# Two tile pools change places in SBUF, and six extra tiles move into the larger one

## The chip, the cores and the metric

One NeuronCore of a Trainium2 chip. The metric is the device time of one execution, in microseconds (us). PE is the TensorE (PEld its weight loads), DVE the VectorE, ACT the ScalarE, POOL the GpSimd, SP the SyncE.

## The reference

Two layers on a sequence of 512 tokens of 1024 channels. Each layer is a SwiGLU feed-forward network (FFN) at half weight, a mixer (causal pooling in the first layer, multi-head latent attention in the second), and another such FFN. The four FFNs are most of the work:

```python
def swiglu(h, w_gate, w_up, w_down):
    return (jax.nn.silu(h @ w_gate) * (h @ w_up)) @ w_down
...
    for i in range(DEPTH):
        h = rmsnorm(x, ffn1_norm[i])
        x = x + FFN_HALF * swiglu(h, ffn1_w_gate[i], ffn1_w_up[i], ffn1_w_down[i])
        h = rmsnorm(x, mix_norm[i])
        ...
        h = rmsnorm(x, ffn2_norm[i])
        x = x + FFN_HALF * swiglu(h, ffn2_w_gate[i], ffn2_w_up[i], ffn2_w_down[i])
```

D_MODEL is 1024, D_FF 2816, everything float32.

## The kernel before

**Arithmetic.** A float32 product is made of three matmuls in float32r: each operand is split into a high part (ACT, L117) and a low part (DVE, L118), and `mm3` issues high x high, high x low and low x high (L110 to L112, all through the helper at L106). In `mm(ps, lhsT, rhs)` the first operand is the stationary one (128x128, loaded by an LDWEIGHTS before each matmul) and the second is the moving one, 256, 384 or 512 columns wide. A trace row names both: in `acc<-slot,hi` the moving operand is a tile `slot`, the stationary one a tile `hi`.

**FFN.** The 22 column tiles of gate and up are worked in four chunks (4, 6, 6, 6). Chunk 0 multiplies plainly, with 512 moving columns, and so do all down projections and the mixers' input and output projections. In chunks 1 to 3 a pair of column tiles and a pair of halves of the tokens are multiplied as 2x2 blocks with seven products instead of eight (class `Two`). Each product is 12 matmuls of 256 columns: four slices k of the channels, three matmuls each. Their numbers in the code are 1 to 7, and their order in one round is 5, 1, 4, 7, 6, 3, 2 (`twos`).

**Where the operands of the seven products stand.** Moving: the normalized activations `xn` and their block sums `ts`, high and low, 32 tiles of 128x512 in all, of which 26 are tiles `slot` of the pool `sp`. The other six come from `extra()` (L307): tiles named `t` in the FFN's own pool `fp`, for `xn[7]` and for the sums of k = 0. So products 7, 6, 5 and 4 begin with three matmuls whose moving operand is a `t`, and products 3 and 2 end with three. Stationary: the high and low parts for products 1, 2, 5 and 6 stand in the pool `wp` (tags `whi`, `wlo`), those for 3, 4 and 7 in `fp` (tags `chi`, `clo`, `dhi`, `dlo`). All other products have weights from `wp` and moving operands from `sp`, or, in the pooling layer and the attention, the other way about.

**Where the pools stand.** A pool takes a stretch of each SBUF partition in the order in which the pools are opened. The program as built has these offsets, in bytes of a partition; the last column is the remainder of the matmul operands' offsets by 512:

| pool | what | from | to | remainder by 512 |
|---|---|---|---|---|
| `sp` | 39 tiles `slot`, 2048 B each | 22944 | 102816 | 416 |
| `wp` | `raw`, `whi`, `wlo`, three tiles of 4096 B each | 102816 | 139680 | 416 |
| `kp`, `tp` | work tiles, small tiles (2884 B of them) | 139680 | 163044 | |
| `fp` | FFN's own: `s`, `chi`, `clo`, `m`, `t`, `dhi`, `dlo`, `z` | 163072 | 228608 | 256 |
| `mp` (instead of `fp` in the attention) | `vhi`, `vlo` and others | 163072 | 213984 | 480 for `vhi`, `vlo` |

The slices inside a tile are multiples of 512 B, so a matmul's operand has its tile's remainder.

Of the kernel before, what the change touches and what calls it, by code (L numbers as in the profile page):

```python
# [10 lines left out]
F32R = mybir.dt.float32r  # L11
# [7 lines left out]
P = 128  # L19
D = 1024  # L20
S = 512
FF = 2816
KD = D // P
# [54 lines left out]
def trunk(ctx: ExitStack, tc: tile.TileContext, a: dict, out: bass.AP):  # L78
# [1 line left out]

    cp = ctx.enter_context(tc.tile_pool(name="cp", bufs=1))
    xp = ctx.enter_context(tc.tile_pool(name="xp", bufs=1))
    sp = ctx.enter_context(tc.tile_pool(name="sp", bufs=39))
    wp = ctx.enter_context(tc.tile_pool(name="wp", bufs=3))
    kp = ctx.enter_context(tc.tile_pool(name="kp", bufs=2))
    tp = ctx.enter_context(tc.tile_pool(name="tp", bufs=2))
    pa = ctx.enter_context(tc.tile_pool(name="pa", bufs=6, space=PSUM))
    pb = ctx.enter_context(tc.tile_pool(name="pb", bufs=2, space=PSUM))

# [6 lines left out]
    def slot(shape=None):  # L96
        return sp.tile(shape or [P, S], F32R, tag="slot", name="slot")
# [16 lines left out]
    def split(src, hi, lo, scale=None):  # L114

        if scale is None:
            nc.scalar.activation(hi, src, AF.Copy)  # L117
            nc.vector.tensor_tensor(out=lo, in0=src, in1=hi.bitcast(F32), op=ALU.subtract)  # L118
        else:
            nc.scalar.activation(hi, src, AF.Copy, scale=scale)  # L120
            nc.vector.scalar_tensor_tensor(  # L121
                out=lo, in0=src, scalar=scale, in1=hi.bitcast(F32), op0=ALU.mult, op1=ALU.subtract
            )

    def load_w(src, cols):
        raw = wp.tile([P, WC], F32, tag="raw", name="raw")
        hi = wp.tile([P, WC], F32R, tag="whi", name="whi")
        lo = wp.tile([P, WC], F32R, tag="wlo", name="wlo")
        nc.sync.dma_start(raw[:, :cols], src)
        split(raw[:, :cols], hi[:, :cols], lo[:, :cols])  # L130
        return hi, lo
# [129 lines left out]
    def ffn(n, layer, prep, nxt, first=False, final=False):  # L261
        wg, wu, wd = (a[f"ffn{n}_{k}"] for k in ("gate", "up", "down"))
        with tc.tile_pool(name="fp", bufs=1) as fp:
            ffn_in(fp, wg[layer], wu[layer], wd[layer], prep, nxt, first, final)

    def ffn_in(fp, wg, wu, wd, prep, nxt, first, final):
# [37 lines left out]

        xn, ts, kept = [None] * KD, {}, []

        def extra():  # L307
            return fp.tile([P, S], F32R, tag="t", name="t", bufs=6)

        def normed(k):  # L310

            tag, dt = (("s", F32), ("s", F32), ("chi", F32R), ("clo", F32R))[k]
            both = fp.tile([P, 2 * S], dt, tag=tag, name=tag, bufs=2)
            both = both.bitcast(F32) if dt is F32R else both
            kept.append(both)
            for e, j in enumerate((k, KH + k)):
                t = both[:, e * S : (e + 1) * S]
                nc.vector.scalar_tensor_tensor(
                    out=t, in0=xs[j], scalar=gains[:, prep.gcol + j : prep.gcol + j + 1],
                    in1=rows, op0=ALU.mult, op1=ALU.mult,  # L320
                )
                xn[j] = (extra(), extra()) if j == KD - 1 else (slot(), slot())
                split(t, *xn[j])

        def x_sums(k):

            b12, b11, b22, b21 = (kept[k][:, c * C : (c + 1) * C] for c in range(4))
            t = fp.tile([P, 4 * C], F32, tag="m", name="m", bufs=2)
            t1, t2, t3, t4 = (t[:, c * C : (c + 1) * C] for c in range(4))
            for out, x, y in ((t1, b12, b11), (t2, b22, t1), (t3, b22, b12), (t4, b21, t2)):  # L330
                nc.vector.tensor_tensor(out=out, in0=x, in1=y, op=ALU.subtract)
            for e in range(2):
                new = extra if k == 0 else slot
                hi, lo = new(), new()
                split(t[:, e * S : (e + 1) * S], hi, lo)
                ts[k, 2 * e] = hi[:, :C], lo[:, :C]
                ts[k, 2 * e + 1] = hi[:, C:], lo[:, C:]
# [119 lines left out]
        for f0, f1 in CHUNKS:  # L457
            hs = []
            for f in range(f0, min(f1, 4), 2):
                if first and f == 0:  # L460
                    pg, pu = opening(wg[0], wu[0], prep)
                else:
                    pg = product(wg[f], xh)
                    if f == 0:
                        prep.squares()
                    if f == 2:
                        normed(0)
                    pu = product(wu[f], xh)
                    if f == 2:
                        normed(1)  # L470
                if rows is None:
                    r = prep.rstd()
                qg = product(wg[f + 1], xh)
                if rows is None:
                    rows = prep.rstd_rows(r)
                zs = scaled(pg), scaled(pu)
                if f == 2:
                    normed(2)
                hs.append(gated([(slice(0, S), zs[0])], zs[1]))
                qu = product(wu[f + 1], xh)  # L480
                if f == 2:
                    x_sums(0)
                zs = scaled(qg), scaled(qu)
                if f == 2:
                    normed(3)
                hs.append(gated([(slice(0, S), zs[0])], zs[1]))
# [9 lines left out]
            for m in range(KD):  # L496
                if f0 == 0 and m % 2 and m > 1:
                    x_sums(m // 2)
                hi, lo = load_w(wd[m][:, f0 * P : f1 * P], nf * P)

                nc_ = 2 if final and f1 == NFT and m == KD - 1 else 1
                for e in range(nc_):
                    p = acc()
                    cs = slice(e * S // nc_, (e + 1) * S // nc_)
                    for f in range(nf):
                        fs = slice(f * P, (f + 1) * P)
                        h = hs[f][0][:, cs], hs[f][1][:, cs]
                        mm3(p[:, cs], (hi[:, fs], lo[:, fs]), h, f == 0, f == nf - 1)
                    nc.vector.scalar_tensor_tensor(  # L509
                        out=xs[m][:, cs], in0=p[:, cs], scalar=0.5, in1=xs[m][:, cs],  # L510
                        op0=ALU.mult, op1=ALU.add,
                    )
                    if final and f1 == NFT:
                        nc.sync.dma_start(out[m][:, cs], xs[m][:, cs])
                if f1 == NFT and not final:
                    nxt.add(m)
# [669 lines left out]
```

## Time and profile before

| | |
|---|---|
| median of 3 runs | 1661.75 us (1661.46 to 1661.96) |
| the profiled execution's own time | 1661.68 us |
| its span, first to last instruction | 1659.9 us |
| granted TensorE clock over the span | 1.00 (2.4 GHz) |
| PE busy | 1649.3 us, 99% of the span |

A matmul's duration in the profile reaches from its start to a modelled end, and consecutive matmuls overlap. So the pace is read from the starts: the time from one matmul's start to that of a later one, divided by the matmuls between. "Pace" has that meaning below.

### The profile page before, as it was taken

Reading aid. Unit: us, or ns where it says so; the run is one execution under the profiler, and the core shown is the slowest. Engines: PE = TensorE matmul, PEld = TensorE weight load, DVE = VectorE, ACT = ScalarE, POOL = GpSimd, SP = SyncE. Lnnn points to the kernel's source line nnn. Section 1 sums busy time; section 2 is a strip of 40 time slices with the busy share of each in tenths; the row PEclk is TensorE's granted clock in tenths of the full one; section 3 lists DMA queues with packets and bytes.
Section 4 is the critical chain, followed back from the end, with each engine's and each line's share of the span. In section 5 each row is a group of like instructions: output and inputs, shape, how many; then the busy total and the mean of one; then the engine's idle time right before and its main releaser. Section 6 shows DMA issues by size and latency. Waiting matters only on the chain.

```text
span 1659.9 us, 26442 instructions
## 1 busy us (share of the span) xinstructions
PE 1649.3 (99%) x10534; PEld 1497.7 (90%) x10534; DVE 1246.0 (75%) x2082; ACT 823.6 (50%) x1411; POOL 47.6 (3%) x133
## 2 busy tenths in 40 slices
PE   8999999999999999999999999999999999999999
PEld 6898999988898989988999999888888889999898
DVE  8985758799976757669858677656778799677673
ACT  6453535455553535445535445446765455445351
POOL 0000000000000000000000000003321000000000
PEclk9999999999999999999999999999999999999999
DMA  5333333231434233332333333331112223333432
GB/s 167 104 116 111 100 89 118 84 114 57 121 102 118 85 112 99 98 96 83 124 92 115 89 115 96 103 88 53 45 58 77 76 65 127 90 115 96 121 90 89
DMA packets 52827, 161.74 MB, mean 97 GB/s; under 512 B 6240, under 2 KB 7008, under 8 KB 52704
## 3 DMA queue, kind: packets, MB, share of 16 engines
q1 hardware_dynamic: 52128, 159.34, 31.9%
q8 instruction: 82, 1.34, 0.3%
q10 hardware_dynamic: 576, 0.72, 0.1%
q14 instruction: 41, 0.34, 0.1%
HBM read 157.94 MB, written 2.10 MB: 96 GB/s over the span
## 4 chain that ended last, share of the span: by engine, by line
PE 95%; DVE 3%; ACT 1%; DMA 1%; issue 0%; SPq 0%; POOL 0%; ACTq 0%; DVEq 0%; POOLq 0%
PE acc L106 92%; PE aux L700 1%; PE aux L106 1%; DVE wlo L118 1%; PE aux L981 1%; DVE x L509 0%; DVE slot L121 0%; DVE sqacc L182 0%; DMA x<-in_xT 0%; DVE s L354 0%; DMA raw<-in_ffn_gate 0%; DMA raw<-in_ffn_up 0%; DMA freq<-in_freq 0%; ACT whi L117 0%; ACT work L962 0%
## 5 line engine op out<-in xcount | busy, mean ns | idle before, releaser
L106 PE MATMUL acc<-slot,whi 128*128 128x512 f32 x2204 | 679.5, 390 | 5.2 <-ACT whi L117 5.1
L106 PE MATMUL acc<-slot,hi 128*128 128x256 f32 x3168 | 582.2, 281 | 0.0
L106 PEld LDWEIGHTS acc<-slot,hi 128*128 128x128 f32 x3168 | 491.8, 190 | 0.9
L106 PEld LDWEIGHTS acc<-slot,whi 128*128 128x128 f32 x2204 | 411.0, 188 | 89.7 <-ACT whi L117 5.5
L106 PE MATMUL acc<-slot,lo 128*128 128x256 f32 x1584 | 446.4, 282 | 0.0
L106 PE MATMUL acc<-slot,wlo 128*128 128x512 f32 x1094 | 425.5, 389 | 0.0
L117 ACT ACTIVATE whi<-raw 128x768 fp32r<-128x768 f32 (+2 forms) x197 | 169.3, 862 | 300.4 <-PE acc L106 205.0
L106 PEld LDWEIGHTS acc<-slot,lo 128*128 128x128 f32 x1584 | 300.1, 189 | 0.1
L118 DVE TENSOR_TENSOR wlo<-raw,whi 128x768 fp32r<-128x768 f32 (+2 forms) x196 | 190.8, 977 | 102.1 <-ACT whi L117 99.8
L106 PEld LDWEIGHTS acc<-slot,wlo 128*128 128x128 f32 x1094 | 205.8, 188 | 43.3 <-DVE wlo L118 1.3
L118 DVE TENSOR_TENSOR lo<-s,hi 128x1024 fp32r<-128x1024 f32 x144 | 175.8, 1221 | 65.4 <-ACT hi L117 65.4
L117 ACT ACTIVATE hi<-raw 128x512 fp32r<-128x512 f32 (+1 forms) x144 | 121.3, 845 | 136.8 <-PE acc L106 84.1
L117 ACT ACTIVATE hi<-s 128x1024 fp32r<-128x1024 f32 x144 | 152.2, 1058 | 65.6 <-PE acc L106 59.4
L509 DVE SCALAR_TENSOR_TENSOR x<-acc,x 128x512 f32<-128x512 f32 x129 | 88.3, 684 | 127.5 <-PE acc L106 127.4
L106 PE MATMUL acc<-t,hi 128*128 128x256 f32 x864 | 171.4, 283 | 0.1
L118 DVE TENSOR_TENSOR lo<-raw,hi 128x1024 fp32r<-128x1024 f32 (+1 forms) x144 | 137.0, 951 | 4.5 <-ACT hi L117 4.4
L397 ACT ACTIVATE m<-acc 128x256 f32<-128x256 f32 x216 | 82.3, 382 | 116.7 <-PE acc L106 116.6
L106 PEld LDWEIGHTS acc<-t,hi 128*128 128x128 f32 x864 | 133.0, 189 | 2.3 <-ACT m L397 2.3
L106 PE MATMUL acc<-t,lo 128*128 128x256 f32 x432 | 122.0, 283 | 0.0
L354 DVE TENSOR_TENSOR s<-raw 128x512 f32<-128x512 f32 x144 | 96.3, 687 | 16.7 <-DMA raw<-in_ffn_up 12.1
L106 PE MATMUL acc<-whi,slot 128*128 128x384 f32 (+2 forms) x320 | 87.6, 344 | 0.0
L440 DVE TENSOR_TENSOR z<-acc,m 128x256 f32<-128x256 f32 (+1 forms) x144 | 79.6, 552 | 8.6 <-PE acc L106 7.5
(185 smaller groups left out, 1445.5 us busy)
## 6 DMA issues: line engine op xcount, KB each, us to landing
raw<-in_ffn_gate SPq DMA_DIRECT2D x87, 512.0 KB, 3.5
raw<-in_ffn_up SPq DMA_DIRECT2D x87, 512.0 KB, 3.6
raw<-in_ffn_down SPq DMA_DIRECT2D x96, 384.0 KB, 3.3
raw<-in_ffn_down SPq DMA_DIRECT2D x32, 256.0 KB, 2.7
raw<-in_w_q SPq DMA_DIRECT2D x12, 384.0 KB, 3.1
raw<-in_w_in SPq DMA_DIRECT2D x8, 512.0 KB, 3.5
raw<-in_w_out SPq DMA_DIRECT2D x8, 512.0 KB, 3.6
x<-in_xT SPq DMA_DIRECT2D x8, 256.0 KB, 5.2
```

What stands on the lines that cost most here:

```text
L106: nc.tensor.matmul(ps, lhsT, rhs, start=start, stop=stop, skip_group_check=skip)
L117: nc.scalar.activation(hi, src, AF.Copy)
L118: nc.vector.tensor_tensor(out=lo, in0=src, in1=hi.bitcast(F32), op=ALU.subtract)
L354: nc.vector.tensor_tensor(out=out, in0=x, in1=y, op=op)
L397: nc.scalar.activation(self.kept[:, c[(1, 6, 7).index(n)]], part, AF.Copy)
L440: nc.vector.tensor_tensor(out=out, in0=x, in1=y, op=ALU.add)
L509: nc.vector.scalar_tensor_tensor(out=xs[m][:, cs], in0=p[:, cs], scalar=0.5, in1=xs[m][:, cs], op0=ALU.mult, op1=ALU.add,)
L700: nc.tensor.transpose(p[:, i * P : (i + 1) * P], src(i), ident)
L981: nc.tensor.transpose(p[:, js], self.pr[i][:, js], ident)
```

## The change

It opens `sp` with 45 tiles instead of 39 and takes the six extra tiles of each FFN from there, and it opens `wp` after `kp` and `tp`.

```diff
-    sp = ctx.enter_context(tc.tile_pool(name="sp", bufs=39))
-    wp = ctx.enter_context(tc.tile_pool(name="wp", bufs=3))
+    sp = ctx.enter_context(tc.tile_pool(name="sp", bufs=45))
     kp = ctx.enter_context(tc.tile_pool(name="kp", bufs=2))
     tp = ctx.enter_context(tc.tile_pool(name="tp", bufs=2))
+    wp = ctx.enter_context(tc.tile_pool(name="wp", bufs=3))
...
-        def extra():
-            return fp.tile([P, S], F32R, tag="t", name="t", bufs=6)
-
...
-                xn[j] = (extra(), extra()) if j == KD - 1 else (slot(), slot())
+                xn[j] = slot(), slot()
...
-                new = extra if k == 0 else slot
-                hi, lo = new(), new()
+                hi, lo = slot(), slot()
```

The pools then stand so:

| pool | from | to | remainder by 512 |
|---|---|---|---|
| `sp` | 22944 | 115104 | 416 |
| `kp`, `tp` | 115104 | 138468 | |
| `wp` | 138496 | 175360 | 256 |
| `fp` | 175360 | 228608 | 256 |
| `mp` (instead of `fp` in the attention) | 175360 | 226272 | 480 for `vhi`, `vlo` |

PE's 10,520 program rows keep their order and shapes; the operands' tiles differ. First place: PE in the first FFN, where a product 4 begins (`hi_1732` is the high part of its weights, in `fp`). Before:

```order
L106 MATMUL acc_1737<-t_528,hi_1732 128x256
L106 MATMUL acc_1737<-t_529,hi_1732 128x256
L106 MATMUL acc_1737<-t_528,lo_1733 128x256
L106 MATMUL acc_1737<-slot_622,hi_1732 128x256
L106 MATMUL acc_1737<-slot_623,hi_1732 128x256
L106 MATMUL acc_1737<-slot_622,lo_1733 128x256
```

Now:

```order
L106 MATMUL acc_1737<-slot_528,hi_1732 128x256
L106 MATMUL acc_1737<-slot_529,hi_1732 128x256
L106 MATMUL acc_1737<-slot_528,lo_1733 128x256
L106 MATMUL acc_1737<-slot_622,hi_1732 128x256
L106 MATMUL acc_1737<-slot_623,hi_1732 128x256
L106 MATMUL acc_1737<-slot_622,lo_1733 128x256
```

Nothing moved in the order; the first three moving operands come from `sp`, at offset 41376 for `slot_528`, where `t_528` stood at 195840. By all matmuls of the program: of the 6,468 that have 256 float32r columns, 1,944 had a moving operand of remainder 416 and a stationary one of remainder 256, and now 6,084 have; of the 3,398 of 512 columns none had, and now 3,262 have.

Second place: ACT in chunk 0 of the first FFN, where the sums of k = 0 (`m_519`) are split into the tiles that were `t`. Before:

```order
L117 ACTIVATE whi_554<-raw_553 128x512
L117 ACTIVATE t_524<-m_519 128x512
L117 ACTIVATE slot_484<-work_467 128x512
L117 ACTIVATE t_528<-m_519 128x512
L117 ACTIVATE whi_574<-raw_573 128x512
L117 ACTIVATE slot_538<-clo_536 128x512
L117 ACTIVATE t_543<-clo_536 128x512
```

Now:

```order
L117 ACTIVATE whi_554<-raw_553 128x512
L117 ACTIVATE slot_484<-work_467 128x512
L117 ACTIVATE slot_524<-m_519 128x512
L117 ACTIVATE slot_528<-m_519 128x512
L117 ACTIVATE whi_574<-raw_573 128x512
L117 ACTIVATE slot_538<-clo_536 128x512
L117 ACTIVATE slot_543<-clo_536 128x512
```

One split moved behind its neighbour. That happens in three of the FFNs: 6 rows of ACT and 21 of DVE stand at another place, all in this stretch; PE, POOL and SP have every instruction where it was.

## Rows read from the trace of the kernel before

**Rows 1.** Profile page, parts 1 and 2: busy us; granted clock in 40 slices

```profile
PE 1649.3 (99%) x10534; PEld 1497.7 (90%) x10534; DVE 1246.0 (75%) x2082; ACT 823.6 (50%) x1411; POOL 47.6 (3%) x133
...
PEclk9999999999999999999999999999999999999999
```

**Rows 2.** Waits of PE: us in total, times, longest

```profile
PE acc L106 <- ACT whi L117: 5.1, 1, 5.1
PE aux L981 <- POOL work L967: 0.7, 1, 0.7
```

**Rows 3.** PE's matmuls by form: xcount | busy us, mean ns | idle

```profile
L106 PE MATMUL acc<-slot,whi 128*128 128x512 f32 x2180 | 675.1, 391 | 5.2 <-ACT whi L117 5.1
L106 PE MATMUL acc<-slot,hi 128*128 128x256 f32 x3168 | 582.2, 281 | 0.0
L106 PE MATMUL acc<-slot,lo 128*128 128x256 f32 x1584 | 446.4, 282 | 0.0
L106 PE MATMUL acc<-slot,wlo 128*128 128x512 f32 x1082 | 422.1, 390 | 0.0
L106 PE MATMUL acc<-t,hi 128*128 128x256 f32 x864 | 171.4, 283 | 0.1
L106 PE MATMUL acc<-t,lo 128*128 128x256 f32 x432 | 122.0, 283 | 0.0
```

**Rows 4.** Timeline of PE, one round of seven products: start us, us, matmul

```profile
176.90 0.40 PE L106 MATMUL acc<-t,hi 128*128 128x256 f32 x2
...
177.25 0.40 PE L106 MATMUL acc<-slot,hi 128*128 128x256 f32 x2
...
178.32 0.40 PE L106 MATMUL acc<-t,hi 128*128 128x256 f32 x2
...
178.68 0.40 PE L106 MATMUL acc<-slot,hi 128*128 128x256 f32 x2
...
179.74 0.41 PE L106 MATMUL acc<-t,hi 128*128 128x256 f32 x2
...
181.18 0.40 PE L106 MATMUL acc<-slot,hi 128*128 128x256 f32 x2
...
182.23 0.40 PE L106 MATMUL acc<-t,hi 128*128 128x256 f32 x2
...
182.59 0.39 PE L106 MATMUL acc<-slot,hi 128*128 128x256 f32 x2
...
184.01 0.40 PE L106 MATMUL acc<-t,hi 128*128 128x256 f32 x2
...
185.45 0.40 PE L106 MATMUL acc<-slot,hi 128*128 128x256 f32 x2
...
186.89 0.28 PE L106 MATMUL acc<-t,hi 128*128 128x256 f32 x1
```

**Rows 5.** Timeline of PE, 512 columns wide, opening FFN

```profile
26.57 0.39 PE L106 MATMUL acc<-slot,wlo 128*128 128x512 f32 x1
...
27.96 0.39 PE L106 MATMUL acc<-slot,wlo 128*128 128x512 f32 x1
...
56.98 0.41 PE L106 MATMUL acc<-slot,whi 128*128 128x512 f32 x1
```

**Rows 6.** Timeline of PE, attention's values, moving slots, stationary `vhi`, `vlo`

```profile
1200.31 0.39 PE L106 MATMUL acc<-slot,vhi 128*128 128x256 f32 x2
...
1201.33 0.34 PE L106 MATMUL acc<-whi,slot 128*128 128x384 f32 x1
```

**Rows 7.** Tile `t`: instructions, min/median/max ns, first and last start us

```profile
L106 PE MATMUL acc<-t,hi x864: 277/282/386, 77.7 to 1623.5; 128*128 128x256 f32 x173
...
L118 DVE TENSOR_TENSOR t<-m,t x8: 682/684/687, 45.3 to 1349.1; 128x512 fp32r<-128x512 f32 x8
```

## Prediction

> **What bounds the kernel now.** I read the page first: PE is busy for 1649.3 of 1659.9 us at a granted clock of full speed in all 40 slices [rows 1]. Then PE's waits: the longest is 5.1 us, once, the next 0.7 us, and the other four are shorter still [rows 2]. So no wait and no clock step is left to win or lose; the time is the sum of the paces of some ten thousand matmuls. By form, two kinds make up nearly all of it: 2180 + 1082 = 3262 matmuls of 512 columns with a moving `slot` and weights from `wp`, and 3168 + 1584 + 864 + 432 = 6048 of 256 columns, those of the seven products [rows 3]. The durations there overlap and say little, so I went to the timeline for paces.
>
> In the seven products, one round (4, 7, 6, 3, 2, 5, 1) begins at 176.90 and the next product 4 at 186.89: 9.99 us for 84 matmuls, a pace of 118.9 ns. Its products are not equal, though each is 12 matmuls of one shape: 4, 7 and 3, with weights from `fp`, take 1.42, 1.42 and 1.41 us, while 6, 5 and 1, with weights from `wp`, take 1.44 us each (182.59 to 184.01 gives 1.42 for product 2) [rows 4]. Product 1 has only `slot` as moving operand and takes 1.44 us, 120 ns a matmul. At 2.4 GHz 256 columns are 106.7 ns and 512 are 213.3 ns (an estimate: one column a cycle). So product 1 has 13.3 ns a matmul over its columns. In the plain products the timeline has 128 matmuls from 27.96 to 56.98 us, a pace of 226.7 ns, and that again is 13.3 ns over the columns [rows 5]. Both have moving and stationary tiles of remainder 416. I call this the settled pace: an overhead per matmul, the same for both widths.
>
> The overhead is not fixed by shape alone. In the attention, nine matmuls of 256 columns with moving slots and weights of remainder 480 go from 1200.31 to 1201.33 us, 113.3 ns each, 6.7 ns over the columns [rows 6]. And stretches with only moving slots and weights from `fp` (416 against 256) go at other paces again: the last nine of product 4 take 178.32 - 177.25 = 1.07 us (118.9 ns), the last nine of product 7 179.74 - 178.68 = 1.06 us (117.8), the first nine of product 3 182.23 - 181.18 = 1.05 us (116.7) [rows 4]. Their mean is 117.8 ns, 11.1 ns over the columns. The pairing of places sets the overhead, and this pairing is the one that the change gives to nearly every matmul.
>
> **The change part by part.** *Weights of products 1, 2, 5 and 6 at remainder 256, `t` into slots.* All 6048 matmuls get the pairing that has run at 117.8 ns (116.7 to 118.9) against 118.9 now. That is 1.1 ns x 6048 = 6.7 us less; the bounds are nothing and 2.2 x 6048 = 13.3 us. I take the mean, since each of the three stretches stands for one of the three products that have this pairing now.
>
> *Weights of the 3262 matmuls of 512 columns at remainder 256.* The trace has no such matmul of this width. The nearest row for the pairing is that of 256 columns, 11.1 ns of overhead (10.0 to 12.2). In the settled state the overhead did not grow with the width, so I carry it over: 213.3 + 11.1 = 224.4 ns against 226.7, 2.3 ns less, times 3262 is 7.5 us less (3.6 to 10.8). The other bound, upward, comes from the one stretch where 512 columns run unsettled: right after a wait, six matmuls from 26.57 to 27.96 us go at 231.7 ns [rows 5]. By that 3262 matmuls would cost 5.0 ns more each, 16.3 us. I take the value for the pairing and keep the upper one for a rival.
>
> *Moves on ACT and DVE, 27 rows.* They are splits in chunk 0 whose results PE first reads much later: the low part of `t` is written from 45.3 us, and the first matmul with a `t` starts at 77.7 us [rows 7]. That 32 us is the cover. What is queued behind a split on ACT is a split of weights; a neighbour pair that changes places leaves it where it was. No instruction was added, and SP's transfers keep their order. I count nothing; without the cover, one DVE split of 0.68 us in each of three FFNs would be 2 us.
>
> *Pooling and attention.* 480 matmuls with moving weights of `wp` and stationary slots change their pairing as well, to 256 against 416. Three nanoseconds each way, the spread between the pairings above, would be 1.4 us. I count nothing.
>
> Sum against the profiled execution's own 1661.7 us, which is the median of the runs within 0.1 us: 1661.7 - 6.7 - 7.5 = 1647.5, rounded to 1648. With both bounds the same way the forecast's own range is 1638 to 1658; I write 1640 to 1657.
>
> **A rule that speaks against it.** Product 1 and the slots of product 3 have one shape and one clock and differ by 3 ns a matmul [rows 4]. The Trainium skill, SBUF — State Buffer, section "Who interferes with whom", says that PE never waits on anyone at SBUF, and TensorE: Matmul & The Clock Gate, section "Step-by-step: what each phase is for", that loading the next weights takes no read bandwidth from the running matmul. By those two the place of a tile could not matter and the time would stay at 1661.7; the row does not agree with them for 256 columns, and for 512 no row can say.
>
> **The rivals.**
>
> *Nothing changes.* The differences between the products could come from their place in the round and not from their operands. Against it: within a product they follow the pairing. For it: 3 ns are small, and the stretches have nine matmuls only. The time is then 1661.7 us.
>
> *Only the seven products gain.* The settled overhead of 13.3 ns at 512 columns could be a state that any undisturbed run reaches, whatever the pairing; the run of 128 did so [rows 5]. Then 1661.7 - 6.7 = 1655 us.
>
> *Everything settles at 120 ns (slower).* Where the operands' places change, as between product 5 and 1 or 1 and 4, the settled pace has to form anew; product 1 is the undisturbed one at 120 ns. After the change nothing differs between products any more, so all 6048 could settle at 120 ns: 1.1 ns x 6048 = 6.7 us more, 1668 us. Against it: the slots' stretches in products 3 and 7 show no approach to 120 in nine matmuls. It decides above 119.5 ns for the round, where the loss passes 0.2%.
>
> *512 columns do not settle (slower).* With this pairing the 256-column stretches vary from 116.7 to 118.9 ns, so they are not settled; wide matmuls that are not settled run at 231.7 ns. Then 1661.7 - 6.7 + 16.3 = 1671 us. It decides above 226.7 + 6.7 us / 3262 = 228.8 ns. For it: it is the only row of unsettled wide matmuls. Against it: that stretch follows a wait, which nothing in the change repeats.
>
> **How the numbers follow.** A measurement of this kernel can tell about 0.2% from no change, 3.3 us. The forecast has 0.38, "only the seven products" 0.14: faster 0.52. "Nothing changes" has 0.12: same 0.12. "512 columns do not settle" has 0.26 and "everything settles at 120" 0.10: slower 0.36. Signs on both sides hold most of the chance, so the range has to reach from the forecast's 1640 to the slow rival's 1671 and a little over, 1673; what is left out is its outer bounds and mixtures beyond them.
>
> **What would show it right or wrong.** In the profile after, the pace of the undisturbed 512-column run (the same 128 matmuls from the end of the opening to the first wait) decides first: 224 to 225 ns is the forecast, 226.7 the second rival, 231 or more the last. A round of seven products should take 9.90 us, with the products of `wp` weights as fast as those of `fp` weights; 10.08 us is the settling rival. No `t` may be left among the matmuls, PE's waits should stay near 6 us in all, and the clock at full speed. Wrong altogether would be a time change that stands in PE's waits, or a matmul pace that stays as it was while the time moves.

## The result and the profile after

The changed kernel takes 1676.77 us (median of 4 runs, 1676.56 to 1677.07), the kernel before 1661.68 us beside it: a ratio of 1.0088 (95% interval 1.0076 to 1.0100), slower by 15.1 us. The forecast was 1648 us, the range 1640 to 1673. In the experiments below one run of the first (2406.38 us) and one of the kernel before beside it (2718.71 us) stand far from all others, and the intervals and ranges leave them out.

The profile page of the changed kernel, parts 1 and 2, against [rows 1]:

```profile
PE 1664.9 (99%) x10534; PEld 1494.1 (89%) x10534; DVE 1247.4 (74%) x2082; ACT 823.8 (49%) x1411; POOL 47.4 (3%) x133
...
PEclk9999999999999999999999999999999999999999
```

Its waits of PE (us in total, times, longest), against [rows 2]:

```profile
PE acc L106 <- ACT whi L117: 5.0, 1, 5.0
PE aux L977 <- POOL work L963: 0.7, 1, 0.7
```

Its matmuls by form (count, busy us, mean ns, idle), against [rows 3]:

```profile
L106 PE MATMUL acc<-slot,hi 128*128 128x256 f32 x4032 | 716.3, 280 | 0.0
L106 PE MATMUL acc<-slot,whi 128*128 128x512 f32 x2180 | 690.2, 398 | 5.0 <-ACT whi L117 5.0
L106 PE MATMUL acc<-slot,lo 128*128 128x256 f32 x2016 | 564.2, 280 | 0.0
L106 PE MATMUL acc<-slot,wlo 128*128 128x512 f32 x1082 | 429.7, 397 | 0.0
```

PE was busy for 1649.3 us and is busy for 1664.9: the whole 15 us is time in which TensorE works. Clock and waits stayed. The forms show where: the narrow matmuls became shorter by 1 to 3 ns (281 to 283 before, 280 now), the wide ones longer by 7 (391 and 390 before, 398 and 397 now). No tile `t` is left among the matmuls.

The paces come from the timeline of PE (start us, us, matmul): the run of 128 wide matmuls that [rows 5] has before, two rounds of seven products (the round of [rows 4], and one of a later stretch), and the attention's values of [rows 6].

```profile
26.47 0.39 PE L106 MATMUL acc<-slot,wlo 128*128 128x512 f32 x1
27.86 0.39 PE L106 MATMUL acc<-slot,wlo 128*128 128x512 f32 x1
...
57.84 0.39 PE L106 MATMUL acc<-slot,whi 128*128 128x512 f32 x1
...
179.07 0.40 PE L106 MATMUL acc<-slot,hi 128*128 128x256 f32 x2
...
189.04 0.40 PE L106 MATMUL acc<-slot,hi 128*128 128x256 f32 x2
...
272.86 0.40 PE L106 MATMUL acc<-slot,hi 128*128 128x256 f32 x2
...
282.72 0.40 PE L106 MATMUL acc<-slot,hi 128*128 128x256 f32 x2
...
1211.60 0.39 PE L106 MATMUL acc<-slot,vhi 128*128 128x256 f32 x2
...
1212.62 0.34 PE L106 MATMUL acc<-whi,slot 128*128 128x384 f32 x1
```

The 128 wide ones take 57.84 - 27.86 = 29.98 us, 234.2 ns each, where they took 226.7. They never settle: the six behind the wait go at 231.7 ns as before, and what follows is slower than they are. The round at 179.07 takes 9.97 us (118.7 ns a matmul; 118.9 before), the one at 272.86 takes 9.86 (117.4). The attention's values, whose places by 512 did not change, take 1.02 us as before.

Summed from start to start over all such matmuls of the two traces, the 3262 wide ones take 22.5 us more, the 6048 narrow ones 7.2 us less, and all others together 0.2 us less: 15.1 us.

### The profile page after: what moved, and what is told of

The parts are those of the page before. It is cut to its first block, busy times and chain, and to the rows that moved or that the text cites. A ratio compares the mean times of both kernels' runs of the same rounds, so it can differ in the third digit from the quotient of the medians.

```text
span 1674.9 us, 26445 instructions
## 1 busy us (share of the span) xinstructions
PE 1664.9 (99%) x10534; PEld 1494.1 (89%) x10534; DVE 1247.4 (74%) x2082; ACT 823.8 (49%) x1411; POOL 47.4 (3%) x133
## 4 chain that ended last, share of the span: by engine, by line
PE 98%; ACT 0%; DVE 0%; DMA 0%; issue 0%; POOL 0%; ACTq 0%; POOLq 0%
PE acc L106 96%; PE aux L696 1%; PE aux L106 1%; PE aux L977 0%; DMA gains<-in_gains 0%; ACT work L958 0%; DVE wlo L118 0%; ACT slot L117 0%; ACT slot L120 0%; ACT whi L117 0%; POOL work L963 0%; ACT work L846 0%; DVE small L952 0%; DVE small L158 0%; DVE slot L118 0%
## 5 line engine op out<-in xcount | busy, mean ns | idle before, releaser
L106 PE MATMUL acc<-slot,hi 128*128 128x256 f32 x4032 | 716.3, 280 | 0.0
L106 PE MATMUL acc<-slot,whi 128*128 128x512 f32 x2204 | 694.5, 397 | 5.0 <-ACT whi L117 5.0
L106 PEld LDWEIGHTS acc<-slot,hi 128*128 128x128 f32 x4032 | 618.4, 188 | 3.6 <-ACT m L393 2.5
L106 PE MATMUL acc<-slot,lo 128*128 128x256 f32 x2016 | 564.2, 280 | 0.0
L106 PE MATMUL acc<-slot,wlo 128*128 128x512 f32 x1094 | 433.1, 396 | 0.0
L106 PEld LDWEIGHTS acc<-slot,lo 128*128 128x128 f32 x2016 | 379.4, 188 | 0.0
L117 ACT ACTIVATE slot<-z 128x512 fp32r<-128x512 f32 x72 | 43.4, 619 | 35.8 <-DVE z L429 35.8
L106 PEld LDWEIGHTS acc<-whi,slot 128*128 128x128 f32 x320 | 57.0, 188 | 2.9 <-ACT whi L117 0.4
L106 PE MATMUL acc<-wlo,slot 128*128 128x384 f32 (+2 forms) x160 | 54.9, 345 | 0.3 <-DVE wlo L118 0.3
```

The costliest lines, as they stand in the source:

```text
L106: nc.tensor.matmul(ps, lhsT, rhs, start=start, stop=stop, skip_group_check=skip)
```

## The experiments

Two readings stood against each other. The first: the pace of a matmul is set by how its two operands stand to each other in SBUF, that is by the place of its weights minus the place of its moving operand. Below this is called the *difference*, in bytes; moving at 416 and weights at 256 is 256 - 416 = -160, a difference of 352 by the remainders modulo 512. The rival: it is not the remainders but something else that the change brought (the distance of the pools, the region of SBUF, the six tiles, or what DVE and ACT do beside).

**Undoing the remainder alone.** The change stays, and two paddings put the weights of `wp` back to remainder 416, in the upper region of SBUF; `fp` stays at 256.

```diff
+    pad1 = ctx.enter_context(tc.tile_pool(name="pad1", bufs=1)).tile([P, 40], F32, name="pad1")
     wp = ctx.enter_context(tc.tile_pool(name="wp", bufs=3))
+    pad2 = ctx.enter_context(tc.tile_pool(name="pad2", bufs=1)).tile([P, 88], F32, name="pad2")
```

> The changed kernel with 160 bytes of unused room ahead of the weights' pool and 352 behind it: the weights stay in the upper part of SBUF, but their remainder by 512 is 416 again, that of the slots; the pool of the FFN keeps 256. Theory of remainders (the pace follows the remainders by 512 of the two operands, not where they stand otherwise): 512 columns return from 234 to 226.7 ns, the products with weights in the weights' pool go to 120, so the time falls to about 1659 us (1655 to 1664). Rival, distance (weights farther up in SBUF cost the wide matmuls): stays at 1677. Rival, the six tiles in slots are the cause: stays at 1677.

It took 1660.86 us, 0.9992 of before (0.9982 to 1.0002). Its 128 wide matmuls in the timeline of PE:

```profile
28.51 0.39 PE L108 MATMUL acc<-slot,wlo 128*128 128x512 f32 x1
...
57.55 0.40 PE L108 MATMUL acc<-slot,whi 128*128 128x512 f32 x1
```

29.04 us, 226.9 ns. The loss is gone with 160 bytes of padding ahead of `wp` (the 352 behind it only keep `fp` at its remainder), so neither the region nor the distance nor the six tiles made it.

**The remainder alone, in the kernel before.** The kernel before with a padding of 352 bytes ahead of `wp` and one of 160 behind `tp`: only the weights of `wp` go from 416 to 256.

```diff
     sp = ctx.enter_context(tc.tile_pool(name="sp", bufs=39))
+    pad1 = ctx.enter_context(tc.tile_pool(name="pad1", bufs=1)).tile([P, 88], F32, name="pad1")
     wp = ctx.enter_context(tc.tile_pool(name="wp", bufs=3))
...
     tp = ctx.enter_context(tc.tile_pool(name="tp", bufs=2))
+    pad2 = ctx.enter_context(tc.tile_pool(name="pad2", bufs=1)).tile([P, 40], F32, name="pad2")
```

> The kernel before with 352 bytes of unused room ahead of the weights' pool and 160 behind the small tiles: no pool changes its order, the tiles t stay, only the weights' remainder becomes 256. Theory of remainders: 512 columns rise to 234 ns, 3262 x 7.3 = 24 us, the products save some 3 us, so about 1682 us (1677 to 1686). Rivals distance and six tiles: as before, 1662.

1679.13 us, 1.0102 (1.0085 to 1.0119). The same run of wide matmuls:

```profile
28.77 0.40 PE L108 MATMUL acc<-slot,wlo 128*128 128x512 f32 x1
...
58.76 0.39 PE L108 MATMUL acc<-slot,whi 128*128 128x512 f32 x1
```

29.99 us, 234.3 ns. So the loss comes without the rest of the change: the moving slots stand where they did, and `fp` stands 512 bytes higher, at its old remainder.

**The other half of the change alone.** 45 slots and no `t`, with `wp` left directly behind `sp`.

```diff
     sp = ctx.enter_context(tc.tile_pool(name="sp", bufs=45))
+    wp = ctx.enter_context(tc.tile_pool(name="wp", bufs=3))
     kp = ctx.enter_context(tc.tile_pool(name="kp", bufs=2))
     tp = ctx.enter_context(tc.tile_pool(name="tp", bufs=2))
-    wp = ctx.enter_context(tc.tile_pool(name="wp", bufs=3))
```

> Half of the change: 45 slots and no tile t, but the weights' pool directly behind the slots as before (it begins 12288 bytes later, remainder 416 as before). Theory of remainders: 512 columns stay at 226.7 ns, the time is that of the first kernel of this call within 2 us, about 1659 (1655 to 1664). Rival six tiles: 1677. Rival distance: about 1662.

1660.93 us, 0.9992 (0.9982 to 1.0001): within what can be told from no change. What the six tiles do is worth at most a microsecond or two.

**All weights 64 bytes above the slots.** The pairing at which [rows 6] has 113.3 ns, given to everything by 224 bytes of padding ahead of `wp` (remainder 480).

> The changed kernel with 224 bytes of unused room ahead of the weights' pool: all weights, in both pools, get the remainder 480, 64 above the slots', the pairing that the attention's values had at 113.3 ns. Theory of remainders: the 6048 matmuls of 256 columns go from 117.8 to 113.3 ns, 27 us less; for 512 columns the bounds are 234 (no change) and 213.3 + 6.7 = 220 ns (46 us less): 1604 to 1650 us. Rivals distance and six tiles: 1677.

1661.84 us, 0.9992 (0.9982 to 1.0001), single runs from 1655.70 to 1663.70, a wider scatter than that of the kernel before beside it (1661.21 to 1663.15), and above the 1604 to 1650 expected. The timeline of PE, the wide run and a round:

```profile
29.72 0.39 PE L107 MATMUL acc<-slot,wlo 128*128 128x512 f32 x1
...
59.59 0.39 PE L107 MATMUL acc<-slot,whi 128*128 128x512 f32 x1
...
179.76 0.39 PE L107 MATMUL acc<-slot,hi 128*128 128x256 f32 x2
...
189.28 0.39 PE L107 MATMUL acc<-slot,hi 128*128 128x256 f32 x2
```

The round takes 9.52 us, 113.3 ns a matmul, as hoped; the wide matmuls go at 29.87 / 128 = 233.4 ns. Again a pairing that is better at 256 columns is worse at 512. And the 113.3 ns hold in under half of the narrow matmuls only: of the kernel's twelve stretches of seven products five settle at it and seven at 117.8 ns, at the same difference.

**A map.** Matmuls alone, without the rest of the kernel, over all differences in steps of 32 bytes.

```diff
+    for n, xc, wc in CHAINS:    # columns, place of the moving operand, place of the weights
...
+                for m, (i, j) in enumerate(((0, 0), (0, 1), (1, 0))):
+                    nc.tensor.matmul(p[:, :n], ws[i], xs[j], start=k == 0 and m == 0, stop=k == 7 and m == 2)
```

> A kernel that holds nothing of the computation: 64 chains of 72 float32r matmuls on TensorE with nothing running beside them, 256 columns in the first 32 chains and 512 in the others, moving operand at remainder 416 (of its place in the partition, modulo 512 bytes) in 16 chains and at 0 in the next 16, and the weights 0, 32, ..., 480 bytes further on. If the pace is set by the two remainders alone, the chains at moving 416 give what the kernels gave: weights at the same remainder 120 ns at 256 columns and 226.7 at 512, weights 352 further 117.8 and 234.2, weights 64 further 113.3 and 233.3; and if only the difference counts, moving at 0 gives the same 16 values again. If what VectorE and ScalarE do beside the matmuls makes the pace, the chains don't show these differences, and all differences give one pace for each width.

The timeline of PE in windows inside single chains: 256 columns at differences 96, 192 and 256, then 512 columns at 0, 96, 128 and 192. A row merges all matmuls of the window: start of the first, us to the end of the last, count.

```profile
37.24 7.20 PE L106 MATMUL acc<-x,w 128*128 128x256 f32 x60
...
62.76 7.11 PE L106 MATMUL acc<-x,w 128*128 128x256 f32 x59
...
79.74 7.48 PE L106 MATMUL acc<-x,w 128*128 128x256 f32 x61
...
284.74 14.44 PE L106 MATMUL acc<-x,w 128*128 128x512 f32 x63
...
333.75 14.45 PE L106 MATMUL acc<-x,w 128*128 128x512 f32 x61
...
350.62 14.57 PE L106 MATMUL acc<-x,w 128*128 128x512 f32 x62
...
383.69 14.60 PE L106 MATMUL acc<-x,w 128*128 128x512 f32 x63
```

The end of the last matmul is modelled, 0.28 us (0.40 when wide) behind its start, so a pace is for example (7.20 - 0.28) / 59 = 117.3 ns. All chains by their starts, once past the first matmuls (ns):

| difference | 0 | 32 | 64 | 96 | 128 | 160 | 192 | 224 |
|---|---|---|---|---|---|---|---|---|
| 256 columns | 120.0 | 118.3 | 117.8 | 117.4 | 118.6 | 120.0 | 117.8 | 117.8 |
| 512 columns | 226.7 | 233.3 | 233.3 | 234.2 | 232.4 | 233.3 | 228.9 | 233.3 |

Differences of 256 and more repeat the table, and so does a moving operand at remainder 0: only the difference counts, modulo 256. The change's 352 is 96 here: the best of the table at 256 columns, the very worst at 512. With nothing running beside TensorE the kernel's paces come out again, so the rival about DVE and ACT falls too. One thing did not fit: 64 gives 117.8 here and nowhere the 113.3 ns of the kernel.

**The same difference behind different work.** A second map at 256 columns, in steps of 16 bytes, behind three kinds of other matmuls.

> A kernel that holds nothing of the computation: 48 chains of 96 matmuls of 256 columns, moving at remainder 416 and weights 0, 16, ..., 240 bytes further on, each behind 24 other matmuls: of 512 columns with weights at the moving remainder in the first 16, of 512 columns at the chain's own difference in the next 16, of 128 columns in the last 16. In the map before, weights 64 further went at 117.8 ns, in the kernel with all weights 64 further long stretches at 113.3. If a pairing has one pace, all three entries give 117.8 at 64. If it has two and the matmuls ahead choose, the chains behind 512 columns at the chain's own difference show 113.3 at 64 as the kernel did, and the others may not; other differences may show a second pace as well.

Windows in the timeline of PE: difference 64 behind 512 columns at difference 0 and behind 128 columns, 96 behind the same two, then 192 behind 512 columns at difference 0 and at 192.

```profile
84.22 10.53 PE L106 MATMUL acc<-x,w 128*128 128x256 f32 x88
...
610.45 10.48 PE L106 MATMUL acc<-x,w 128*128 128x256 f32 x91
...
117.78 10.49 PE L106 MATMUL acc<-x,w 128*128 128x256 f32 x88
...
638.23 10.49 PE L106 MATMUL acc<-x,w 128*128 128x256 f32 x87
...
219.27 10.41 PE L106 MATMUL acc<-x,w 128*128 128x256 f32 x87
...
489.79 10.48 PE L106 MATMUL acc<-x,w 128*128 128x256 f32 x91
```

The pairs read 117.8 and 113.3 ns, 117.4 and 118.7, 117.8 and 113.3. So some differences have two paces, each of which keeps itself up for as long as the chain lasts, and in this map the matmuls ahead choose between them. The changed kernel's two rounds show the two paces of 96: of its twelve stretches of seven products, four settle at 118.7 and eight at 117.3 ns. At 208 all three entries gave 116.7 ns.

In the kernels the matmuls ahead are not all that chooses. For the chain at 64 behind 512 columns at 64 the expectation had 113.3 ns; the map gave 117.8. And in the kernel with all weights 64 above the slots, eleven of the twelve stretches begin at 113.3 ns. After about 50 matmuls the weight loads (PEld) then wait once in each stretch for a copy by ACT (L394), and behind that wait five go at 113.3 ns and seven at 117.8. Its waits of PEld, and the third stretch in the timeline of PE:

```profile
PEld acc L107 <- ACT m L394: 2.7, 12, 0.3
...
262.66 0.39 PE L107 MATMUL acc<-slot,hi 128*128 128x256 f32 x2
...
268.10 0.80 PE L107 MATMUL acc<-slot,hi 128*128 128x256 f32 x3
...
268.85 0.40 PE L107 MATMUL acc<-slot,hi 128*128 128x256 f32 x2
...
278.63 0.40 PE L107 MATMUL acc<-slot,hi 128*128 128x256 f32 x2
```

Ahead of the wait 48 matmuls take 5.44 us, 113.3 ns; behind it 83 take 9.78 us, 117.8 ns. The round at 179.76 above belongs to the second stretch, which came out of its wait at 113.3. The wait was 217 ns long in six of the seven stretches that went on slowly, and 219 or 220 in four of the five quick ones; no run tests whether that is what decides.

The second map also holds a difference that is quick at both widths. At 240 the wide matmuls ahead of the chain settle at 226.7 ns, as at 0, and the chain goes at 117.3 ns behind all three entries:

```profile
535.17 3.79 PE L106 MATMUL acc<-x,w 128*128 128x512 f32 x16
...
539.72 10.48 PE L106 MATMUL acc<-x,w 128*128 128x256 f32 x88
```

No run puts a whole kernel at 240.

**All weights at a difference of 192**, the second best at 512 columns, by 96 bytes of padding ahead of `wp`.

> The changed kernel with 96 bytes of padding ahead of wp, so that all weights stand at remainder 352, 64 below the slots, which is a difference of 192 modulo 256. By the maps 512 columns go at 228.8 ns there (7 us more than before over 3262 matmuls) and 256 columns at one of two paces, 113.3 or 117.8 ns (34 or 7 us less over 6048). If the maps carry over to the kernel: 1635 us where the quick state holds throughout, 1662 where it never does, something between where waits throw it from one to the other. If the maps of two operands in isolation miss what the kernel's other engines do, 512 columns are not at 228.8.

1658.48 us, 0.9979 (0.9970 to 0.9989). Wide matmuls at 229.0 ns on the mean of all pairs, narrow at 117.6. Behind wide matmuls at 192 the second map had the quick pace, 113.3 ns; here only five of the twelve stretches begin at it, and from the wait on ACT's copy on all twelve go at 117.8. The small gain is what the map gives without the quick pace.

**Each width at its own difference.** The wide matmuls at 0, those of the products 1, 2, 5 and 6 moved by 208 bytes inside their tiles; those of 3, 4 and 7, in `fp`, come to 224, where the second map has 116.7 or 117.8. The tiles are 256 bytes larger, and one `work` tile makes room.

```diff
-        return kp.tile(shape or [P, S], F32, tag="work", name="work", bufs=7)
+        return kp.tile(shape or [P, S], F32, tag="work", name="work", bufs=6)
...
-        hi = wp.tile([P, WC], F32R, tag="whi", name="whi")
+        hi = wp.tile([P, WC + 64], F32R, tag="whi", name="whi")
...
-                hi = pool.tile([P, n], F32R, tag=tag + "hi", name="hi", bufs=bufs)
+                o = SHIFT if pool is wp else 0
+                m = n + 64 if pool is wp else n
+                hi = pool.tile([P, m], F32R, tag=tag + "hi", name="hi", bufs=bufs)[:, o : o + n]
```

> The changed kernel with wp at the slots' remainder for the matmuls of 512 columns, and the weights of products 1, 2, 5 and 6 placed 208 bytes inside their wp tiles (which are 256 bytes larger), those of products 3, 4 and 7 at a difference of 224 modulo 256. To make room, the work tiles are 6 instead of 7. By the maps: 512 columns at 226.7 to 227.1 ns as before, 256 columns at 116.7 ns at 208 behind any entry, and at 116.7 or 117.8 at 224: 2.2 ns less than before over 6048 matmuls, or 1.8, so 1648 to 1651 us. If six work tiles are too few, PE's waits grow beyond the 6 us of before and the time with them.

1648.40 us, 0.9919 (0.9904 to 0.9934). The timeline of PE, the wide run and a round:

```profile
27.45 0.39 PE L109 MATMUL acc<-slot,wlo 128*128 128x512 f32 x1
...
56.47 0.41 PE L109 MATMUL acc<-slot,whi 128*128 128x512 f32 x1
...
175.16 0.40 PE L109 MATMUL acc<-slot,hi 128*128 128x256 f32 x2
...
184.96 0.40 PE L109 MATMUL acc<-slot,hi 128*128 128x256 f32 x2
```

226.7 ns, and 9.80 us a round, 116.7 ns: both as the maps have them. PE's longest wait is 5.1 us as before, so the sixth `work` tile cost nothing that shows.

**The same at 192.**

> As the run with 208, with a difference of 192 for all seven products; matmuls of 512 columns stay at difference 0. By the second map 256 columns behind 512 columns at difference 0 go into the pace of 117.8 ns, 1.1 less than before, 1655 us. If waits of TensorE throw the sequence into the pace of 113.3, as they did in the kernel with all weights 64 above the slots, it goes down to 1628 us; between the two in proportion to the share of matmuls at each pace.

1654.87 us, 0.9959 (0.9945 to 0.9973), every narrow stretch at 117.8 ns. Behind wide matmuls at difference 0 the slow one of the two paces is entered, as the second map had it; the quick one was never seen.

**The same at 64.**

> As the run with 208, with a difference of 64 for the seven products; 512 columns stay at 0. The second map has two paces at 64: 117.8 behind 512 columns, 113.3 behind 128 columns. If the chain stays in the pace it enters with, 117.8 ns throughout and 1655 us, as at 192. If waits throw it into the other, as in the kernel with all weights 64 above the slots (115.7 on the mean), down to 1642 us at that mean, and 1628 at 113.3 throughout.

1648.70 us, 0.9917 (0.9896 to 0.9938), single runs from 1645.48 to 1652.65. In the trace about 15% of the narrow matmuls run at 113.3 ns and the rest at 117.8: all twelve stretches begin at 117.8, and two leave the wait at 113.3.

**64, and a push.** In each of the twelve stretches one narrow matmul is made as two of 128 columns, some 20 matmuls behind the wait on ACT's copy. The work is the same.

```diff
+                    if parted and k == KH - 1 and e == 2:
+                        for h in (slice(0, P), slice(P, C)):
+                            mm(p[:, h], w[i][:, ks], xk(k)[j][:, h], False, False, skip=True)
+                        continue
```

> The run with 64 and one disturbance in each of the twelve stretches of seven products: the last matmul of the first product 1 behind the opening four is made as two of 128 columns (24 such in the program, about 0.1 us more each pair). If narrow matmuls ahead throw the chain into the pace of 113.3, the five sixths of each stretch behind them run at 113.3 instead of 117.8: 4.5 ns x 5000 = 22 us below the run without, 1632 us against 1655. If one pair does not do it, the time is that of the run without plus 1 to 2 us.

1634.35 us, 0.9834 (0.9820 to 0.9849), single runs from 1633.98 to 1635.31. The timeline of PE around the second stretch's pair:

```profile
173.09 0.28 PE L109 MATMUL acc<-slot,lo 128*128 128x256 f32 x1
...
175.09 0.34 PE L109 MATMUL acc<-slot,lo 128*128 128x128 f32 x2
...
176.02 0.39 PE L109 MATMUL acc<-slot,hi 128*128 128x256 f32 x2
...
185.88 0.39 PE L109 MATMUL acc<-slot,hi 128*128 128x256 f32 x2
```

Ahead of the pair 17 matmuls take 2.00 us, 117.6 ns; behind it, after six slower ones, 87 take 9.86 us, 113.3 ns. Of the twelve stretches nine reach the pair at 117.8 ns and three at 113.3; all twelve leave it at 113.3, and ten keep that to their end, while two fall back to 117.8 for their last 5.7 us. Two matmuls of 128 columns changed the pace of the hundreds behind them, at the same places in SBUF. This is 28 us faster than before and 42 us faster than the change.

## Why the prediction was wrong

**The step that failed** is the term of the 3262 wide matmuls, "in the settled state the overhead did not grow with the width, so I carry it over". 224.4 ns was forecast, 234.2 came: 22.5 us more in place of 7.5 less. The step rested on one pairing that had been seen at both widths, difference 0, where the 13.3 ns over the columns are indeed the same at 120.0 and 226.7 ns. The map shows that 0 is the only one of its eight differences at which this holds. At 96 the overhead is 10.7 ns at 256 columns and 20.9 at 512. So a rule was drawn from the one case that keeps it.

**The bound** was too low as well. The 231.7 ns of six matmuls behind a wait were taken as the price of "not settled", but they are a way back to the settled pace and say nothing of another pairing's own pace: 234.2 ns lies above them. The rival "512 columns do not settle" had the place, the sign and the condition (it decides above 228.8 ns); its 5.0 ns a matmul were 7.2, and its 1671 us left the range's end below the result.

**The narrow term** was right: 6.7 us forecast, 7.2 measured, with 117.8 ns on the mean of all pairs as forecast. That it came so near is in part luck: the mean is made of two paces, eight stretches at 117.3 and four at 118.7, while the forecast's three rows of nine matmuls (116.7, 117.8 and 118.9) were taken for the scatter of one pace. The rival "everything settles at 120 ns" did not come: that is what difference 0 does.

**The parts counted at nothing** were nothing: the moved splits of ACT and DVE left no wait, and pooling and attention moved by 0.2 us in all. The rival "nothing changes" and the second one fall with the wide run, which is neither at 226.7 nor unmoved.

**The rule weighed there** has now been seen at both widths. By the Trainium skill, SBUF — State Buffer, section "Who interferes with whom", TensorE reads the moving operand and the weights through two independent ports and waits on nobody. The runs do not agree with it: padding alone, 160 bytes ahead of `wp` and 352 behind it, makes the wide matmul 226.9 instead of 234.2 ns.

What stays open is the mechanism. That the difference counts modulo 256 bytes is shown, and so is that a chain keeps its pace until a wait or other matmuls disturb it. Why the difference counts, and what decides which pace a wait leaves behind, no run here looked at.

## What to carry to other kernels

Where TensorE is busy throughout, the places of a matmul's operands are a cost of their own, here 3 to 6% of a matmul: look at the starts in the timeline for each pair of pools and each width, and carry a pace from one width to another only if rows show it for that pairing. A microbenchmark of chains of matmuls over all differences takes one run. It forecasts a whole kernel to within a few microseconds where the paces of a difference were one or lay close (208 and 224: 1648 to 1651 expected, 1648.40 measured). Where it showed two, it gave only bounds (192 throughout: 1635 to 1662 expected, 1658.48 measured). When single runs of a kernel scatter more than they used to, look for stretches of the same matmuls at two paces, and for the matmuls and the short waits ahead of each.

## What the hardware did that was not expected

- The pace at a given pairing depends on the difference of the places modulo 256 bytes: at 512 columns from 226.7 (0) over 228.9 (192) to 234.2 ns (96), at 256 columns for example 120.0 (0 and 160) and 116.7 ns (208).
- Some differences have two paces that each keep themselves up: 113.3 and 117.8 ns at 64 and 192, 117.4 and 118.7 at 96. Matmuls ahead can choose, and so can a wait of the weight loads of 0.2 us. One pair of matmuls of 128 columns is enough: 1634.35 us with twelve such pairs against 1648.70 without.
- In chains at a difference of 0, matmuls of 128 columns in float32r were no quicker than those of 256: 112 ns between their starts against 113 to 120.
